# One comparison for four tokens' one-hot rows, and first products queued behind the gate products of their group

## The chip, the cores and the metric

The kernel runs on one core of a Trainium2 chip. The metric is the device time of one launch in microseconds (us). TensorE (PE) multiplies matrices, VectorE (DVE), ScalarE (ACT) and GpSimd (POOL) work on tiles of 128 partitions, and SyncE (SP) issues most of the DMAs.

## The reference, cut to what matters

The program is one step of a decoder layer for 512 prompt tokens and 64 sample tokens. Its first part (projections, a short convolution, windowed attention, a layer norm) is not touched. The part that matters is PEER: each token picks 8 x 16 of 16384 experts, and an expert's number is a pair of keys of 128 each.

```
idx  = cand_i[best]                                # key_a * 128 + key_b, 8 heads x 16 per token
gate = softmax(best_s)
pre  = einsum('nd,nhkd->nhk', xb, expert_u[idx])
coef = gate * gelu(pre)
out  = einsum('nhk,nhkd->nd', coef, expert_v[idx])
```

## The kernel before

The 576 tokens are split. Two tiles of tokens (GATHER) fetch their experts' rows one by one with indirect DMAs. This is the side work: `experts` yields after each of 385 steps, and a step issues a gather of 512 KB on POOL (line 511) and a multiply with a sum on DVE (line 525, tile `junk`; in the later half line 534). Three tiles of 128 tokens (DENSE, 384 tokens) are computed against all 16384 experts, 128 tiles of 128 experts each.

For the dense tokens there are three pieces of work:

- A **front** (function `front`) makes the first product of one expert tile: a 512 KB load, its split into a high and a low part (`whi` on ACT, `wlo` on POOL, lines 118 and 119, four buffers each), 24 matmuls of 384 columns (lines 122 to 124), and a GELU on ACT. For the first 60 tiles the result goes to DRAM (`spill`). Each split also paces the side work: 2, 1, 2, 1, ... steps per front.
- The **gate products** (`gate_matrix`) turn each token's 128 pairs of keys and gates into a matrix of 128 x 128. Keys and gates are transposed into `pt` (line 755), copied to `T`, and for each token two one-hot tiles are made: `oj` marks the second key, `oi` marks the first key times the gate. One matmul `oj` x `oi` (line 775) gives the token's matrix. Four tokens share a PSUM bank, which ACT copies out (line 776), and 16 tokens (a **group**) go to DRAM as `gd` (line 778). `ONE_HOT = "vvag"` lets DVE make `oj` for two of four tokens, ACT for one (two instructions, lines 769 and 770) and POOL for one; DVE makes every `oi` (line 774). `iota_ps` is the row 0 to 127 in PSUM.
- A **back** multiplies a front's result with the gate matrices (`gm` read from `gd`, `re` from `spill`), splits the product (`chi`, `clo`), and adds 18 matmuls to the sums `acc` (line 913).

The keys come out of two top-16 searches on DVE (`top16`, `route`, lines 413 to 472), tile by tile. 20 fronts are queued during these searches. Then 24 groups of gate products follow, and with them the next fronts: 46 of them in equal shares after each group, the last 3 of the first 69 (AHEAD) behind the last gate product. Then the loop over the 128 expert tiles starts: a back for each, and fronts again from the 70th on, which begin once 58 backs are queued. `gm` needs the `gd` of all groups.

Each engine runs its instructions in the order of its queue. The build's scheduler sets that order from its own estimate of times and from the dependences; `tc.issue_after(x)` puts the instructions that are written in its block behind x in the queue of x's own engine, and binds no other engine.

Of the kernel before, what the change touches and what calls it, by code (L numbers as in the profile page):

```python
# [17 lines left out]
AF = mybir.ActivationFunctionType  # L18
ALU = mybir.AluOpType
# [28 lines left out]
GN = 16  # L48
# [5 lines left out]
AHEAD = NS + LAG  # L54
# [1 line left out]
GLAG = 2  # L56
RAW = dict(w=3, v=3)
HI = dict(w=4, v=2)
OB = 10


ORDER = "qkscscasacsca"
FQ = 5
KEEP = 3
LAST = 2


PACE_N = 18
PACE_A, PACE_B, PACE_U, PACE_V = (1, 0), (2, 1, 1), (2, 1), (1, 3)
LO_N = 50  # L70
ONE_HOT = "vvag"


@with_exitstack
def step_kernel(ctx: ExitStack, tc: tile.TileContext, I: dict, O: dict):
    nc = tc.nc
    V, A, G, PE, S = nc.vector, nc.scalar, nc.gpsimd, nc.tensor, nc.sync
# [18 lines left out]
    def bank(tag):  # L96
        if tag == "u":
            return ps_u.tile([128, 512], F32, tag="u", name="ps")
        return pools[tag].tile([128, 512], F32, tag=tag, name="ps")

    def tmp(p, shape, tag, name=None, bufs=1, dt=F32):
        return pools[p].tile(shape, dt, tag=tag, name=name or tag, bufs=bufs)

    loads, newest = [], [None, None]
# [6 lines left out]
    def const(name, shape, dtype=F32, src=None):  # L111
        t = pools["c"].tile(shape, dtype, tag=name, name=name)
        if src is not None:
            loads.append((t, src))
        return t
# [59 lines left out]
    iota128 = const("iota128", [128, 128], src=I["iota128"])  # L175
# [576 lines left out]
    def gate_matrix(i, keys, gt, gd):  # L752
        pt = shared[0]
        for k, src in enumerate((*keys, gt)):
            PE.transpose(pt[:, k * 128:(k + 1) * 128], src, ident)
        iota_ps = pt[:, 384:512]
        T = tmp("k", [128, 3, 128], "T3")
        A.activation(T, pt[:, :384].rearrange("p (k n) -> p k n", k=3), AF.Copy)
        for g in range(128 // GN):
            gb = tmp("b", [128, 128, GN], "gb", bufs=2)  # L760
            for q in range(GN // 4):
                ps = bank("mm")
                for r in range(4):
                    n = g * GN + q * 4 + r
                    oj = tmp("b", [128, 128], "oj", bufs=OB)
                    oi = tmp("b", [128, 128], "oi", bufs=OB)
                    who = ONE_HOT[n % len(ONE_HOT)]
                    if who == "a":
                        A.activation(oj, iota128, AF.Abs, bias=T[:, 1, n:n + 1], scale=-1.0)
                        A.activation(oj, oj, AF.Relu, bias=1.0, scale=-1.0)  # L770
                    else:
                        eng, numbers = (V, iota_ps) if who == "v" else (G, iota128)
                        eng.tensor_scalar(oj, numbers, T[:, 1, n:n + 1], None, op0=ALU.is_equal)  # L773
                    V.tensor_scalar(oi, iota_ps, T[:, 0, n:n + 1], T[:, 2, n:n + 1], op0=ALU.is_equal, op1=ALU.mult)  # L774
                    newest[1] = PE.matmul(ps[:, r * 128:(r + 1) * 128], oj, oi, start=True, stop=True).ins  # L775
                A.activation(gb[:, :, q * 4:(q + 1) * 4].rearrange("p i n -> p n i"),
                             ps.rearrange("p (n i) -> p n i", n=4), AF.Copy)
            S.dma_start(gd[i * (128 // GN) + g], gb)
            yield g

# [48 lines left out]
    def front(t):  # L829
        wu = table(I["euT"][t], "w", G if t < AHEAD else V, PACE_U[t % len(PACE_U)] if t < AHEAD else 0)  # L830
        ps = bank("u")
        for k in range(8):
            mm3(ps[:, :ND], block(wu, k), (hT[0][:, k, :], hT[1][:, k, :]), k == 0, k == 7)
        if t < NS:
            ge = tmp("f", [128, ND], "sp", bufs=2)
            A.activation(ge, ps[:, :ND], AF.Gelu)  # L836
            S.dma_start(spill[t], ge)
        else:
            ge = tmp("f", [128, ND], "gel", bufs=LAG)
            A.activation(ge, ps[:, :ND], AF.Gelu)  # L840
            coef[t] = ge
# [3 lines left out]
    def fronts(n):  # L845
        nonlocal done
        while done < min(n, NE):
            front(done)
            done += 1
# [4 lines left out]
    total = len(DENSE) * 128 // GN  # L854
    base = done
    for i in range(len(DENSE)):
        for g in gate_matrix(i, *second.sel[i], gd):
            fronts(base + (AHEAD - KEEP - base) * (i * (128 // GN) + g + 1) // total)
    with tc.issue_after(newest[1]):
        fronts(AHEAD)  # L860
    bs.close()
# [137 lines left out]
def build(nc, arrays):  # L999
    ins = {k: nc.dram_tensor(f"in_{k}", v.shape, mybir.dt.from_np(v.dtype), kind="ExternalInput").ap()  # L1000
           for k, v in arrays.items()}
    outs = {k: nc.dram_tensor(f"out_{k}", s, F32, kind="ExternalOutput").ap() for k, s in _OUTS.items()}
    with tile.TileContext(nc, schedule_with_timeline_sim=True) as tc:
        step_kernel(tc, ins, outs)
# [20 lines left out]
```

## Time and profile before

| | us |
|---|---|
| median of 3 runs | 1916.29 (1912.41 to 1923.74) |
| the profiled execution | 1920.95 |
| its span in the trace | 1919.2 |
| PE busy in the span | 1752.2 (91%) |
| DVE busy | 1602.6 (84%) |
| POOL busy | 1119.8 (58%) |
| ACT busy | 808.8 (42%) |
| DMA, mean | 259 GB/s |

An engine's busy time counts its compute instructions. Matmuls overlap, so the busy share of PE is above its share of real work, and the step from one matmul's start to the next is the better price. Of the 1.75 us between the span and the execution's time nothing is shown in the trace.

### The profile page before, as it was taken

To read this page: it belongs to the slowest core of one execution; us is meant where nothing else is said; L and a number is where in the kernel's file an instruction comes from. 1 tells how busy PE (TensorE), PEld (TensorE's weight loads), DVE (VectorE), ACT (ScalarE), POOL (GpSimd) and SP (SyncE) were. 2 spreads that over 40 slices of the span, in tenths; PEclk is the share of its full clock that TensorE was granted. 3 is DMA by queue.
4 is the path that set the end of the run, shared out by engine and by line. 5 is a ranking of instruction groups with operands and counts; after the bars stand their busy time and mean duration, and the time that the engine had idled before them with its cause. 6 is when DMAs were issued, how large, how long until landed. Compare 5 with 4: busy or idle time off the path is not lost.

```text
span 1919.2 us, 28284 instructions
## 1 busy us (share of the span) xinstructions
PE 1752.2 (91%) x9760; PEld 1583.2 (82%) x9760; DVE 1602.6 (84%) x3208; ACT 808.8 (42%) x1283; POOL 1119.8 (58%) x724
## 2 busy tenths in 40 slices
PE   8999998988889878789998889999999999999985
PEld 7897897877689778789996677877899999999974
DVE  6646689997956999999999767778888788889888
ACT  4554343433333333466777433333333333343322
POOL 4445434366766656567995222222678777777783
PEclk9999999998989898899998899999999999999998
DMA  6435433347766668668997799999999999989983
GB/s 243 151 127 213 129 131 121 116 169 271 257 204 223 208 203 269 207 228 292 354 355 250 234 334 323 340 348 335 322 339 346 317 336 358 338 312 345 317 270 111
DMA packets 190303, 496.49 MB, mean 259 GB/s; under 512 B 17472, under 2 KB 83456, under 8 KB 187072
## 3 DMA queue, kind: packets, MB, share of 16 engines
q1 hardware_dynamic: 134864, 293.34, 44.5%
q0 software_dynamic: 55296, 201.35, 29.7%
q8 instruction: 77, 1.26, 0.3%
q14 instruction: 66, 0.54, 0.1%
HBM read 454.48 MB, written 40.54 MB: 258 GB/s over the span
## 4 chain that ended last, share of the span: by engine, by line
PE 38%; DVE 31%; DMA 14%; issue 8%; POOL 6%; ACT 2%; SPq 1%; DVEq 0%; POOLq 0%; ACTq 0%
PE acc L913 17%; PE ps L123 6%; PE ps L124 6%; PE ps L122 6%; DVE junk L525 4%; DVE oi L774 4%; POOL wlo L119 3%; POOL g L511 3%; DMA re<-spill 2%; DMA g<-in_eu,idx 2%; DMA g<-in_ev,idx 2%; PE ps L775 2%; DVE oj L773 1%; ACT whi L118 1%; DVE oh L469 1%
## 5 line engine op out<-in xcount | busy, mean ns | idle before, releaser
L119 POOL TENSOR_TENSOR wlo<-raw,whi 128x1024 fp32r<-128x1024 f32 x232 | 580.7, 2506 | 306.6 <-ACT whi L118 277.3
L118 ACT ACTIVATE whi<-raw 128x1024 fp32r<-128x1024 f32 x388 | 409.6, 1056 | 594.1 <-PE ps L123 231.8
L122 PE MATMUL ps<-xhi,whi 128*128 128x384 f32 (+2 forms) x1600 | 534.5, 334 | 24.8 <-ACT sp L836 22.9
L124 PE MATMUL ps<-xhi,wlo 128*128 128x384 f32 (+2 forms) x1600 | 531.9, 333 | 2.6 <-POOL wlo L119 2.6
L123 PE MATMUL ps<-xlo,whi 128*128 128x384 f32 (+2 forms) x1600 | 531.8, 332 | 0.0
L511 POOL DMA_INDIRECT g<-in_eu,idx x192 | 205.9, 1072 | 292.6 <-DVE junk L525 220.3
L534 DVE SCALAR_TENSOR_TENSOR h<-g,pre,h 128x1024 f32<-128x1024 f32 x192 | 315.3, 1642 | 64.8 <-DMA g<-in_ev,idx 63.3
L122 PEld LDWEIGHTS ps<-xhi,whi 128*128 128x128 f32 x1600 | 309.7, 194 | 32.4 <-ACT sp L836 24.5
L511 POOL DMA_INDIRECT g<-in_ev,idx x192 | 259.0, 1349 | 124.4 <-DVE h L534 77.1
L124 PEld LDWEIGHTS ps<-xhi,wlo 128*128 128x128 f32 x1600 | 309.3, 193 | 4.6 <-POOL wlo L119 3.4
L123 PEld LDWEIGHTS ps<-xlo,whi 128*128 128x128 f32 x1600 | 309.3, 193 | 4.3 <-issue 1.4
L913 PE MATMUL acc<-whi,chi 128*128 128x512 f32 x756 | 294.0, 395 | 16.1 <-ACT chi L118 16.1
L913 PE MATMUL acc<-wlo,chi 128*128 128x512 f32 x756 | 299.6, 396 | 6.2 <-POOL wlo L119 6.2
L119 DVE TENSOR_TENSOR wlo<-raw,whi 128x1024 fp32r<-128x1024 f32 x156 | 206.6, 1324 | 58.1 <-ACT whi L118 56.0
L913 PE MATMUL acc<-whi,clo 128*128 128x512 f32 x756 | 251.4, 392 | 2.1 <-DVE clo L119 2.1
L913 PEld LDWEIGHTS acc<-whi,chi 128*128 128x128 f32 x756 | 143.9, 190 | 48.4 <-ACT chi L118 19.7
L913 PEld LDWEIGHTS acc<-wlo,chi 128*128 128x128 f32 x756 | 144.0, 190 | 37.1 <-POOL wlo L119 8.3
L913 PEld LDWEIGHTS acc<-whi,clo 128*128 128x128 f32 x756 | 143.0, 189 | 32.7 <-DVE clo L119 2.7
L775 PE MATMUL ps<-oi,oj 128*128 128x128 f32 x768 | 145.1, 301 | 25.5 <-DVE oi L774 15.0
L775 PEld LDWEIGHTS ps<-oi,oj 128*128 128x128 f32 x768 | 127.9, 202 | 40.2 <-issue 10.6
L525 DVE SCALAR_TENSOR_TENSOR junk<-g,hp 128x1024 bf16<-128x1024 f32 x104 | 125.3, 1205 | 37.6 <-DMA g<-in_eu,idx 35.9
L774 DVE TENSOR_SCALAR oi<-pt,T 128x128 f32<-128x128 f32 x384 | 140.4, 395 | 0.1
(251 smaller groups left out, 2380.8 us busy)
## 6 DMA issues: line engine op xcount, KB each, us to landing
raw<-in_euT SPq DMA_DIRECT2D x128, 512.0 KB
raw<-in_ev SPq DMA_DIRECT2D x128, 512.0 KB
gd<-gb SPq DMA_DIRECT2D x24, 1024.0 KB
gm<-gd SPq DMA_DIRECT2D x48, 512.0 KB
raw<-in_w_g SPq DMA_DIRECT2D x32, 512.0 KB
raw<-in_w_pq SPq DMA_DIRECT2D x32, 512.0 KB
raw<-in_w_bch SPq DMA_DIRECT2D x24, 512.0 KB
spill<-sp SPq DMA_DIRECT2D x60, 192.0 KB
```

The source lines that it names most:

```text
L118: A.activation(hi, src, AF.Copy)
L119: return (eng or V).tensor_tensor(lo, src, hi.bitcast(F32), op=ALU.subtract)
L122: PE.matmul(ps, L[0], R[0], start=start, stop=False)
L123: PE.matmul(ps, L[0], R[1], start=False, stop=False)
L124: PE.matmul(ps, L[1], R[0], start=False, stop=stop)
L469: V.tensor_tensor(oh.rearrange("p h k a -> p (h k) a"), rk.unsqueeze(2).broadcast_to([r, 64, 16]), iota[:r].unsqueeze(1).broadcast_to([r, ...
L511: G.indirect_dma_start(out=rows[i], out_offset=None, in_=I[src], in_offset=bass.IndirectOffsetOnAxis(ap=idx[c][:, s:s + 1], axis=0))
L525: V.scalar_tensor_tensor(junk, g, 1.0, in_psum(c), op0=ALU.mult, op1=ALU.mult, accum_out=p)
L534: V.scalar_tensor_tensor(h_tok[c], g, p, h_tok[c], op0=ALU.mult, op1=ALU.add)
L774: V.tensor_scalar(oi, iota_ps, T[:, 0, n:n + 1], T[:, 2, n:n + 1], op0=ALU.is_equal, op1=ALU.mult)
L775: newest[1] = PE.matmul(ps[:, r * 128:(r + 1) * 128], oj, oi, start=True, stop=True).ins
L913: PE.matmul(*args, **kw)
```

## The change

For every four tokens one DVE comparison of 128 x 1024 makes all eight one-hot rows (`hot`: two keys, four tokens, 128 columns), in place of the one or two DVE instructions per token and the `oj` of ACT and POOL. The gate is then multiplied into the first-key row in place: by ACT for three of four tokens, by POOL for the fourth (`GATED`). DVE takes the copy out of PSUM of the last of a group's four banks (`OUT`). There are three `hot` buffers where there were ten of `oj` and of `oi`. The matmuls of a group's share of fronts stand behind that group's last gate product in PE's queue, and 8 of the first 69 fronts, not 3, stay behind the last gate product.

```diff
--- before.py
+++ after.py
@@ -56,19 +56,20 @@
 GLAG = 2
 RAW = dict(w=3, v=3)
 HI = dict(w=4, v=2)
-OB = 10
+OB = 3
 
 
 ORDER = "qkscscasacsca"
 FQ = 5
-KEEP = 3
+KEEP = 8
 LAST = 2
 
 
 PACE_N = 18
 PACE_A, PACE_B, PACE_U, PACE_V = (1, 0), (2, 1, 1), (2, 1), (1, 3)
 LO_N = 50
-ONE_HOT = "vvag"
+GATED = "aaag"
+OUT = "aaav"
 
 
 @with_exitstack
@@ -760,21 +761,24 @@
             gb = tmp("b", [128, 128, GN], "gb", bufs=2)
             for q in range(GN // 4):
                 ps = bank("mm")
+                n = g * GN + q * 4
+                hot = tmp("b", [128, 2, 4, 128], "hot", bufs=OB)
+                V.tensor_tensor(hot, iota_ps.unsqueeze(1).unsqueeze(1).broadcast_to([128, 2, 4, 128]),
+                                T[:, 0:2, n:n + 4].unsqueeze(3).broadcast_to([128, 2, 4, 128]), op=ALU.is_equal)
                 for r in range(4):
-                    n = g * GN + q * 4 + r
-                    oj = tmp("b", [128, 128], "oj", bufs=OB)
-                    oi = tmp("b", [128, 128], "oi", bufs=OB)
-                    who = ONE_HOT[n % len(ONE_HOT)]
-                    if who == "a":
-                        A.activation(oj, iota128, AF.Abs, bias=T[:, 1, n:n + 1], scale=-1.0)
-                        A.activation(oj, oj, AF.Relu, bias=1.0, scale=-1.0)
+                    oi = hot[:, 0, r, :]
+                    weight_of = T[:, 2, n + r:n + r + 1]
+                    if GATED[r] == "a":
+                        A.activation(oi, oi, AF.Copy, scale=weight_of)
                     else:
-                        eng, numbers = (V, iota_ps) if who == "v" else (G, iota128)
-                        eng.tensor_scalar(oj, numbers, T[:, 1, n:n + 1], None, op0=ALU.is_equal)
-                    V.tensor_scalar(oi, iota_ps, T[:, 0, n:n + 1], T[:, 2, n:n + 1], op0=ALU.is_equal, op1=ALU.mult)
-                    newest[1] = PE.matmul(ps[:, r * 128:(r + 1) * 128], oj, oi, start=True, stop=True).ins
-                A.activation(gb[:, :, q * 4:(q + 1) * 4].rearrange("p i n -> p n i"),
-                             ps.rearrange("p (n i) -> p n i", n=4), AF.Copy)
+                        G.tensor_scalar(oi, oi, weight_of, None, op0=ALU.mult)
+                    newest[1] = PE.matmul(ps[:, r * 128:(r + 1) * 128], hot[:, 1, r, :], oi, start=True, stop=True).ins
+                dst = gb[:, :, q * 4:(q + 1) * 4].rearrange("p i n -> p n i")
+                src = ps.rearrange("p (n i) -> p n i", n=4)
+                if OUT[q] == "a":
+                    A.activation(dst, src, AF.Copy)
+                else:
+                    V.tensor_copy(dst, src)
             S.dma_start(gd[i * (128 // GN) + g], gb)
             yield g
 
@@ -855,7 +859,8 @@
     base = done
     for i in range(len(DENSE)):
         for g in gate_matrix(i, *second.sel[i], gd):
-            fronts(base + (AHEAD - KEEP - base) * (i * (128 // GN) + g + 1) // total)
+            with tc.issue_after(newest[1]):
+                fronts(base + (AHEAD - KEEP - base) * (i * (128 // GN) + g + 1) // total)
     with tc.issue_after(newest[1]):
         fronts(AHEAD)
     bs.close()
```

Three places show what moves. In the order of the program the line numbers after the change are one higher, as far as the gate products.

The first place is PE's queue at the first gate products (`pt` the transposed keys, `oi`, `oj` and `hot` one-hot tiles, 128x384 the matmuls of fronts). Before:

```order
3893 L775 MATMUL ps<-oi,oj 128x128
3894 L122 MATMUL ps<-xhi,whi 128x384
3895 L123 MATMUL ps<-xlo,whi 128x384
3896 L124 MATMUL ps<-xhi,wlo 128x384
3897 L775 MATMUL ps<-oi,oj 128x128 x3
3898 L122 MATMUL ps<-xhi,whi 128x384
3899 L775 MATMUL ps<-oi,oj 128x128
3900 L123 MATMUL ps<-xlo,whi 128x384
3901 L124 MATMUL ps<-xhi,wlo 128x384
3902 L122 MATMUL ps<-xhi,whi 128x384
3903 L775 MATMUL ps<-oi,oj 128x128 x2
```

And in the changed program, from the end of the 20th front on:

```order
3609 L124 MATMUL ps<-xlo,whi 128x384
3610 L125 MATMUL ps<-xhi,wlo 128x384
3611 L756 MATMUL pt<-ident,kk_5506 128x128
3612 L756 MATMUL pt<-ident,kk_5507 128x128
3613 L756 MATMUL pt<-ident,gt 128x128
3614 L775 MATMUL ps<-hot 128x128 x16
3615 L123 MATMUL ps<-xhi,whi 128x384
3616 L124 MATMUL ps<-xlo,whi 128x384
3617 L125 MATMUL ps<-xhi,wlo 128x384
```

Before, 30 of the 69 fronts stand ahead of the last transposes of the first tile, and gate products come singly between the matmuls of fronts. Now 20 fronts stand ahead of them, and the 16 gate products of a group stand together. The further counts are 49 fronts before and 31 now ahead of the second tile's transposes, and 65 and 45 ahead of the third's.

The second place is PE's queue at the last gate products. Before:

```order
4914 L775 MATMUL ps<-oi,oj 128x128
4915 L123 MATMUL ps<-xlo,whi 128x384
4916 L124 MATMUL ps<-xhi,wlo 128x384
4917 L775 MATMUL ps<-oi,oj 128x128 x126
4918 L122 MATMUL ps<-xhi,whi 128x384
4919 L123 MATMUL ps<-xlo,whi 128x384
4920 L124 MATMUL ps<-xhi,wlo 128x384
```

And in the changed program:

```order
4579 L124 MATMUL ps<-xlo,whi 128x384
4580 L125 MATMUL ps<-xhi,wlo 128x384
4581 L775 MATMUL ps<-hot 128x128 x10
4582 L123 MATMUL ps<-xhi,whi 128x384
4583 L124 MATMUL ps<-xlo,whi 128x384
4584 L125 MATMUL ps<-xhi,wlo 128x384
```

Before, 126 gate products of the third tile stand in one piece and 3 fronts behind them; now the last piece is 10 gate products, with 10 fronts behind it (8 kept and the share of the last group). Behind these fronts the 58 backs follow in both.

The third place is DVE's queue in the third tile (`junk` is a step of the side work). Before:

```order
1642 L773 TENSOR_SCALAR oj<-pt,T_10343 128x128
1643 L774 TENSOR_SCALAR oi<-pt,T_10343 128x128
1644 L773 TENSOR_SCALAR oj<-pt,T_10343 128x128
1645 L774 TENSOR_SCALAR oi<-pt,T_10343 128x128 x3
1646 L773 TENSOR_SCALAR oj<-pt,T_10343 128x128
1647 L774 TENSOR_SCALAR oi<-pt,T_10343 128x128
1648 L773 TENSOR_SCALAR oj<-pt,T_10343 128x128
1649 L774 TENSOR_SCALAR oi<-pt,T_10343 128x128 x3
1650 L773 TENSOR_SCALAR oj<-pt,T_10343 128x128
1651 L774 TENSOR_SCALAR oi<-pt,T_10343 128x128
1652 L773 TENSOR_SCALAR oj<-pt,T_10343 128x128
1653 L774 TENSOR_SCALAR oi<-pt,T_10343 128x128
```

And in the changed program:

```order
1267 L766 TENSOR_TENSOR hot<-pt,T_9521 128x1024 x2
1268 L781 COPY gb<-ps 128x4x128
1269 L766 TENSOR_TENSOR hot<-pt,T_9521 128x1024
1270 L526 SCALAR_TENSOR_TENSOR junk,pre<-g,hp 128x1024 x2
1271 L766 TENSOR_TENSOR hot<-pt,T_9521 128x1024 x3
1272 L526 SCALAR_TENSOR_TENSOR junk,pre<-g,hp 128x1024
1273 L781 COPY gb<-ps 128x4x128
1274 L766 TENSOR_TENSOR hot<-pt,T_9521 128x1024
1275 L526 SCALAR_TENSOR_TENSOR junk,pre<-g,hp 128x1024 x2
1276 L766 TENSOR_TENSOR hot<-pt,T_9521 128x1024 x3
1277 L526 SCALAR_TENSOR_TENSOR junk,pre<-g,hp 128x1024
```

Six instructions for four tokens became one; the copy of `gb` waits for the last gate products of its group on PE. Of the side work's DVE steps 77 stand ahead of the first tile's last key reduction before and 69 now; 136 and 125 stand ahead of the last one-hot instruction.

## Rows read from the trace of the kernel before

**Rows 1.** Busy time by stretch: us, PE, PEld, DVE, ACT, POOL, PEclk, DMA share, GB/s.

```profile
727.00:783.00 56.00, 43.45 (x237) 42.50 (x236) 56.00 (x167) 17.45 (x24) 36.21 (x25) 0.92 0.79 259
783.00:913.00 130.00, 117.49 (x711) 113.93 (x712) 130.00 (x339) 80.22 (x138) 90.38 (x71) 0.94 0.73 245
913.00:1008.00 95.00, 95.00 (x640) 95.00 (x639) 90.92 (x251) 71.87 (x129) 86.55 (x77) 1.00 0.96 355
1008.00:1081.00 73.00, 60.03 (x298) 48.87 (x297) 71.02 (x216) 52.98 (x105) 35.12 (x45) 0.88 0.63 227
1081.00:1353.00 272.00, 256.08 (x1113) 210.95 (x1112) 202.69 (x304) 94.83 (x125) 68.69 (x62) 0.97 0.96 333
```

**Rows 2.** Timeline: start us, us, instruction. The marks that end those stretches.

```profile
726.89 0.47 ACT L836 ACTIVATE sp<-ps 128x384 f32<-128x384 f32 x1
...
783.20 0.42 PE L755 MATMUL pt<-ident,gt 128*128 128x128 f32 x1
...
1096.67 0.80 PE L913 MATMUL acc<-whi,chi 128*128 128x512 f32 x1 [3.60 <-ACT chi L118]
...
1353.39 0.33 PE L122 MATMUL ps<-xhi,whi 128*128 128x384 f32 x1
```

**Rows 3.** Timeline of PE: two matmuls 24 apart, and one at the low clock.

```profile
784.38 0.52 PE L122 MATMUL ps<-xhi,whi 128*128 128x384 f32 x1
...
1084.07 0.33 PE L122 MATMUL ps<-xhi,whi 128*128 128x384 f32 x1
...
1088.23 0.33 PE L122 MATMUL ps<-xhi,whi 128*128 128x384 f32 x1
```

**Rows 4.** Timeline of PE: one gate product between two matmuls of a front.

```profile
987.64 0.42 PE L123 MATMUL ps<-xlo,whi 128*128 128x384 f32 x1
987.90 0.39 PE L775 MATMUL ps<-oi,oj 128*128 128x128 f32 x2
988.04 0.42 PE L124 MATMUL ps<-xhi,wlo 128*128 128x384 f32 x1
```

**Rows 5.** Chain that ended last: start us, us. One back's matmuls.

```profile
1707.04 4.12 PE acc L913 x18
```

**Rows 6.** Timeline of PE in the third tile; idle time before, and its releaser, in brackets.

```profile
1058.11 5.51 PE L775 MATMUL ps<-oi,oj 128*128 128x128 f32 x24 [1.00 <-DVE oi L774]
```

**Rows 7.** Groups by line and form: busy us, mean ns | idle before.

```profile
L774 DVE TENSOR_SCALAR oi<-pt,T 128x128 f32<-128x128 f32 x384 | 140.4, 395 | 0.1
L773 DVE TENSOR_SCALAR oj<-pt,T 128x128 f32<-128x128 f32 x192 | 64.2, 334 | 0.9 <-issue 0.9
L773 POOL TENSOR_SCALAR oj<-iota,T 128x128 f32<-128x128 f32 x96 | 63.8, 667 | 40.0 <-PE ps L775 38.7
L769 ACT ACTIVATE oj<-iota,T 128x128 f32<-128x128 f32 x96 | 36.1, 377 | 13.8 <-PE ps L775 13.6
L770 ACT ACTIVATE oj<-oj 128x128 f32<-128x128 f32 x96 | 29.5, 310 | 2.6
L776 ACT ACTIVATE gb<-ps 128x512 f32<-128x512 f32 x96 | 101.6, 1059 | 52.5 <-PE ps L775 48.4 <-issue 2.5 <-PE ps L123 1.6
```

**Rows 8.** Stretches, side-work steps on DVE (L525) alone; two records each.

```profile
783.00:913.00 130.00, 23.44 (x39) 0.94 0.73 245
...
1008.00:1081.00 73.00, 12.94 (x22) 0.88 0.63 227
```

**Rows 9.** Lines L469 and L305 of DVE: ns min/median/max.

```profile
L469 DVE TENSOR_TENSOR oh<-rk,iota x20: 1195/1206/4082, 300.9 to 895.4; 128x1024 bf16<-128x1024 f32 x16, 64x1024 bf16<-64x1024 f32 x4
...
L305 DVE COPY t<-ps x8: 407/666/692, 106.5 to 439.6; 128x512 f32<-128x512 f32 x6, 64x256 f32<-64x256 f32 x2
```

**Rows 10.** Timeline: first and last of six long DVE instructions, and the POOL instruction beside the first.

```profile
740.52 2.88 DVE L457 CAST pf<-pos 128x128 bf16<-128x128 uint32 x1
740.91 2.39 POOL L119 TENSOR_TENSOR wlo<-raw,whi 128x1024 fp32r<-128x1024 f32 x1
...
774.81 3.21 DVE L469 TENSOR_TENSOR oh<-rk,iota 128x1024 bf16<-128x1024 f32 x1
```

## The prediction

> **What bounds the kernel now.** I read the busy times by stretch first, cut at the marks of [rows 2]: 727, where PE is done with the 20th front; 783, the first tile's last transpose; 913 and 1008, the same for the second and third tile; 1081, the last gate product; and 1353, where PE reaches the 70th front. What lies ahead of 727 and behind 1353 has the same queues before and after, so I forecast only how 1353 moves. In [rows 1] no engine bounds all five stretches: DVE is full up to 913, PE and DMA (0.96, 355 GB/s) up to 1008, DVE alone up to 1081, and DMA (0.96) with PE after that. The question in each stretch is how much of it is PE's own work, since PE's work as a whole (49 fronts, 384 gate products, 58 backs) is the same after the change.
>
> Prices on PE: a front is 24 matmuls, and two starts 24 matmuls apart lie 4.16 us apart [rows 3], 0.173 us each. From the start of a front's matmul over a gate product to the next start it is 0.40 us [rows 4], so a gate product costs 0.227 us. A back is 4.12 us [rows 5]. With the counts of fronts from PE's queue, PE's idle or slow time in the five stretches before is:
>
> - 727 to 783: 56 less 10 fronts (41.6) = 14.4.
> - 783 to 913: 130 less 19 fronts (79.0) and 128 gate products (29.1) = 21.9.
> - 913 to 1008: 95 less 16 fronts and 128 products (95.7) = 0.
> - 1008 to 1081: 73 less 1 front and 128 products (33.2) = 39.8. Here PE waits for one-hot tiles of DVE again and again [rows 6].
> - 1081 to 1353: 272 less 3 fronts and 58 backs (12.5 + 239.0) = 20.5.
>
> That is 97 us together. The change can only move this number.
>
> **The change, part by part.**
>
> *One comparison for eight rows.* In the third tile DVE is busy 71.0 us, 12.9 of them for side work [rows 1, 8], so the one-hot tiles take 58.1 us there, 0.454 us a token or 1.82 us for four (less than the mean durations of [rows 7] add up to, since DVE's instructions overlap). A `hot` is not in the trace. The nearest row is the comparison of 128 x 1024 with both operands broadcast, 1.206 us [rows 9]; it reads SBUF alone, and `hot` reads one operand from PSUM. Bounds: 1.1 (0.1 of the row's time saved by overlap) and 1.82 (no gain at all). I take 1.2. So DVE saves 0.6 us for four tokens, 59 us over 96 of them.
>
> *The copies that DVE takes over.* 24 of 96. DVE's copy of the same size out of PSUM takes 0.69 us [rows 9]; ACT's, which writes with the stride of `gb`, 1.06 [rows 7]. Bounds 0.6 and 1.2, taken 0.7: 17 us back on DVE.
>
> *The multiplies.* On POOL 96 multiplies replace 96 comparisons of the same 128 x 128 form at 0.667 us [rows 7]: taken as no change, bounds 0.6 and 0.9. On ACT 288 multiplies with a scale from a column replace 96 pairs of 0.377 and 0.310 us. Between 0.31 and 0.377 each they take 89 to 109 us; less the 66 of the pairs and 25 of the 24 copies, ACT gains or loses between -2 and +18 us. Its cover: ACT was busy 71.9 of 95 us in the busiest stretch [rows 1]. Without cover it would be all of it, 18 us.
>
> *The fronts behind their group.* This moves PE's work and with it loads, splits and side steps. Stretch by stretch:
>
> (a) 727 to the first transposes. PE has only fronts there, and now they may not pass the gate products. So PE stands still from 727 until DVE has the first tile's keys, and DVE decides when that is: it is busy all of the 56 us [rows 1]. Two things leave its way. Eight side steps go behind (77 against 69 in its queue); one costs 23.4 us over some 20 = 1.2 [rows 8], so 9.6 us. And POOL's `wlo` instructions stop once the four buffers are full, since PE frees none. While a `wlo` runs, certain DVE instructions take 2 to 3 us in place of 0.2 to 1.2: the first of them starts just before a `wlo` and ends with it [rows 10]. I count six such in this stretch behind the fourth buffer, 13.5 us over their usual durations. So the keys come at 783 - 9.6 - 13.5 = 760, and PE's idle time is 33 us. Bounds: 28 (DVE also overtakes for want of the other stalls) and 42 (no stall saved but four).
>
> (b) The first tile, 760 on. DVE must still finish the searches. Before it used 130 - 23.4 - 128 x 0.454 = 48.6 us for them in this stretch [rows 1, 8]. Now: 48.6 + 32 `hot` (38.4) + 8 copies (5.6) + 15 side steps (18) = 110.6. PE has 11 fronts and 128 products, 74.9 us, so it idles 36. Bounds 25 (fewer stalls by `wlo`, 11 against about 20) and 50 (`hot` at 1.5 us).
>
> (c) The second and third tile. Now PE has 28 fronts and 256 products, 174.6 us. DVE has 64 x 1.2 + 16 x 0.7 + 41 side steps x 1.2 = 137 us, POOL does for each front and product what it did from 913 to 1008, where it was busy 86.6 of 95 us, and DMA's load is near that of the same stretch. PE should bound this stretch, as it did that one with POOL at 91% and DMA at 0.96 [rows 1]. Its queue is less forgiving, though: no front may fill a wait for the last four tokens of a group. I give it half a microsecond a group, 8 us. Bounds 0 and 30.
>
> So the last gate product lies at 760 + 111 + 183 = 1054, 27 us ahead of 1081.
>
> (d) From there to the 70th front. Ten fronts instead of three: 41.6 + 239.0 = 280.6 us of PE. That covers the way from the last `gd` to the first back, on which PE stood 3.6 us [rows 2] and lost its clock. But DMA is the bound of this stretch: 272 us at 333 GB/s. Seven more fronts' tables and eleven more gathers (136 against 125 steps ahead of the last one-hot instruction), 0.524 MB each, are 9.4 MB or 28 us at that rate, 300 in all if nothing of it was fetched ahead. Between 281 and 300 I take 294: PE idles 13, bounds 1 and 20.
>
> Sum of idle time after: 33 + 36 + 8 + 13 = 90 against 97. The gain is 7 us. Of the 40 us that PE wins back in the third tile most is paid in (a) and (b), where fronts no longer fill the wait for DVE. Against the profiled 1920.95 us this makes 1914; that execution lies 0.24% above the median, so the median comes to 1916.3 x 1914/1920.95 = 1909 us. My own range for this case is 1897 to 1918.
>
> **A rule beside it.** In [rows 3] a matmul takes 0.52 us, not 0.33, right after PE's wait for the transposes: the lower of the two clock levels, 1.2 for 2.4 GHz. In the third tile, where PE got a product every half microsecond, the granted clock stayed at 0.88 [rows 1]. The Trainium skill, "TensorE: Matmul & The Clock Gate", Part 1, says that the slow clock is the default state and that only activity releases it. By that rule a first tile with PE idle a third of the time would run its fronts slow throughout; by the row of the third tile it would not, and the sum goes by the row.
>
> **The rivals.**
>
> 1. *Slower: the last four tokens of each group wait.* The fourth token's multiply stands on POOL behind up to one `wlo` of 2.4 us [rows 10], and PE's fronts stand behind it. At 2.4 us for each of the 16 groups of (c), 38 us in place of 8: 1939. It decides from about 1 us a group on. For it: POOL is 91% busy in the comparable stretch, and three `hot` buffers instead of ten leave little lead. Against: PE runs one or two fronts, 4 to 8 us, between groups, in which three `hot` can be made ready.
> 2. *Slower: the clock falls in (b).* Eleven fronts at twice 4.16 us and products at twice 0.227 make 150 us of PE in place of 111 of DVE, from the point where PE's slow work exceeds DVE's: 1948 in full, some 1930 for half of it. Against: 0.88 in the third tile.
> 3. *Faster: DVE is quicker and DMA no bound.* The stalls by `wlo` shrink in (b) as in (a) and idle time is 25 there, 0 in (c), 2 in (d), 30 in (a): 57, a gain of 40, 1876; half of that 1890. For it: DMA stood at 0.63 in the third tile and at 0.84 just behind it, and could fetch ahead. Against: DMA's 0.96 for 272 us.
> 4. *No change: DMA takes all.* The stretch (d) needs 300 us and nothing is won: 1915.
>
> **How the numbers follow.** A difference under 0.5%, some 9.6 us, is about what a measurement of this kernel cannot tell from none. The forecast case gets 0.43, a little under half of it beyond 0.5% (0.20 faster, 0.23 same). Rival 3 gets 0.22, faster. Rival 4 gets 0.13, same. Rival 1 gets 0.16 and rival 2 0.06, slower. So 0.42 faster, 0.36 same, 0.22 slower. The range of 8 in 10 cuts the far half of rival 3 and the far part of rivals 1 and 2: 1884 to 1935.
>
> **What would show it.** Right: PE without a matmul from 727 to about 760; the first tile's transposes at 760 and the second tile's near 870, with DVE full between; a `hot` near 1.2 us, also while a `wlo` runs; the last gate product near 1054; then 42 us of fronts and the first back without a gap; the 70th front near 1347; DMA at 0.95 or more for the last 290 us of that. Wrong: waits of PE for ACT's or POOL's multiplies in the second and third tile of more than a microsecond a group (rival 1); a granted clock under 0.8 in the first tile (rival 2); DMA well below 0.95 behind the last gate product (rival 3); a `hot` of 1.5 us and more, which adds 10 us in (b) alone.

## The result, and the profile after

The changed kernel takes 1985.03 us (1982.0 to 1992.02, 4 runs) where the kernel before takes 1914.35 on the same chip: a ratio of 1.0382, 95% interval 1.0357 to 1.0407. It is slower by 3.8%, and the prediction, 1909 us, was wrong in sign. The profiled execution took 1983.27 us, its span 1981.5.

Line numbers of the changed program: `hot` is made in L766, the gate is multiplied in by ACT in L772 and by POOL in L774, the product is L775, the copies are L779 (ACT) and L781 (DVE); the lines of the fronts lie one higher than before. The stretches are cut much as in [rows 1], with two differences. The first cut stays at 727 although the mark itself, the spill of the 20th front, lies earlier here, at 720. And the second and third tile are cut at 868 and 992, where the last gate products of the tile ahead end, 4 us behind their transposes (864 and 988). The other cuts are the first tile's transposes (750), the last gate product (1116) and the 70th front.

The busy time by stretch of the changed kernel (us, PE, its weight loads PEld, DVE, ACT, POOL, granted clock of PE, DMA share, GB/s; x counts instructions):

```profile
727.00:750.00 23.00, 0.47 (x1) 0.18 (x1) 23.00 (x115) 0.26 (x1) 0.00 (x0) 0.50 0.06 23
750.00:868.00 118.00, 92.44 (x523) 89.47 (x523) 93.15 (x177) 70.67 (x148) 62.94 (x59) 0.84 0.54 196
868.00:992.00 124.00, 101.98 (x595) 99.65 (x595) 69.19 (x81) 69.64 (x149) 73.40 (x69) 0.92 0.67 238
992.00:1116.00 124.00, 102.01 (x593) 99.86 (x594) 70.16 (x84) 70.01 (x149) 73.27 (x68) 0.91 0.68 241
1116.00:1412.70 296.70, 286.49 (x1286) 242.27 (x1286) 219.59 (x328) 105.13 (x141) 98.01 (x80) 0.98 0.99 344
```

Its timeline has the mark that ends the last of them, the 70th front:

```profile
1412.73 0.33 PE L123 MATMUL ps<-xhi,whi 128*128 128x384 f32 x1
```

Against 1353.39 in [rows 2] that is 59 us later; with 569 us behind the mark (566 before) this is the whole loss of 62 us between the spans. In the two tiles from 868 to 1116 no engine is full: PE 0.82, DVE 0.56, ACT 0.56, POOL 0.59, DMA 0.67. A stretch in which nothing is full is one in which the engines wait for each other in turn. The waits of this stretch say in which order (us in total, times, longest):

```profile
ACT hot L772 <- DVE hot L766: 58.2, 18, 5.5
...
DVE hot L766 <- PE ps L775: 46.5, 11, 6.5
...
PE ps L775 <- ACT hot L772: 40.6, 20, 3.2
...
PE ps L775 <- POOL hot L774: 3.6, 3, 1.2
```

ACT's multiply waits for DVE's comparison, that one for a product of PE, and PE's product for ACT's multiply: a ring. Before, DVE's one-hot instructions waited 1.0 us in all [rows 7]. One turn of it, a group of 16 tokens, on the three engines. PE (fronts left out):

```profile
911.21 1.50 PE L775 MATMUL ps<-hot 128*128 128x128 f32 x12
915.56 4.22 PE L775 MATMUL ps<-hot 128*128 128x128 f32 x20 [2.85 <-ACT hot L772]
```

DVE:

```profile
903.05 1.05 DVE L781 COPY gb<-ps 128x512 f32<-128x512 f32 x1 [1.40 <-PE ps L775]
903.95 1.21 DVE L766 TENSOR_TENSOR hot<-pt,T 128x1024 f32<-128x1024 f32 x1
...
911.70 3.49 DVE L766 TENSOR_TENSOR hot<-pt,T 128x1024 f32<-128x1024 f32 x3 [4.14 <-PE ps L775]
```

ACT:

```profile
912.56 2.78 ACT L779 ACTIVATE gb<-ps 128x512 f32<-128x512 f32 x3
915.14 2.69 ACT L772 ACTIVATE hot<-hot,T 128x128 f32<-128x128 f32 x9
```

A product leaves two records, so PE does 6 products, stands 2.85 us, and does 10. The names with their numbers in PE's queue say which (four `hot` to a group: 8820 to 8856, then 8908 and on; 48 rows of fronts stand at the first dots, 24 at the second):

```
L775 MATMUL ps_8819<-hot_8820 128x128 x3
L775 MATMUL ps_8831<-hot_8832 128x128 x3
...
L775 MATMUL ps_8819<-hot_8820 128x128
L775 MATMUL ps_8831<-hot_8832 128x128
L775 MATMUL ps_8843<-hot_8844 128x128 x4
L775 MATMUL ps_8855<-hot_8856 128x128 x3
L775 MATMUL ps_8907<-hot_8908 128x128 x3
L775 MATMUL ps_8919<-hot_8920 128x128 x3
L775 MATMUL ps_8855<-hot_8856 128x128
...
L775 MATMUL ps_8907<-hot_8908 128x128
```

The first three tokens of `hot` 8820 and 8832 have their products ahead of the share of fronts that is queued behind the group before, the fourth (the one that POOL multiplies) has its product behind it. With three buffers the fourth `hot`, 8856, takes the buffer of 8820, so DVE can only make it when the fronts are over (911.70), and the first two of the next group with it. ACT copies three banks before it multiplies, PE waits, and no front may fill the wait, since the next share is queued behind the group.

### The profile page after: what moved, and what is told of

It reads as the page before. It is cut to its first block, busy times and chain, and to the rows that moved or that the text cites. A ratio compares the mean times of both kernels' runs of the same rounds, so it can differ in the third digit from the quotient of the medians.

```text
span 1981.5 us, 27705 instructions
## 1 busy us (share of the span) xinstructions
PE 1758.6 (89%) x9760; PEld 1597.2 (81%) x9760; DVE 1520.5 (77%) x2752; ACT 807.6 (41%) x1353; POOL 1123.9 (57%) x724
## 5 line engine op out<-in xcount | busy, mean ns | idle before, releaser
L512 POOL DMA_INDIRECT g<-in_ev,idx x192 | 268.5, 1398 | 119.6 <-DVE h L535 72.5
L775 PE MATMUL ps<-hot 128*128 128x128 f32 x768 | 126.7, 327 | 69.0 <-ACT hot L772 65.4
L775 PEld LDWEIGHTS ps<-hot 128*128 128x128 f32 x768 | 118.2, 227 | 76.1 <-ACT hot L772 71.7
L766 DVE TENSOR_TENSOR hot<-pt,T 128x1024 f32<-128x1024 f32 x96 | 113.1, 1212 | 68.1 <-PE ps L775 58.7
```

Source lines behind the costliest of these rows:

```text
L512: G.indirect_dma_start(out=rows[i], out_offset=None, in_=I[src], in_offset=bass.IndirectOffsetOnAxis(ap=idx[c][:, s:s + 1], axis=0))
L766: V.tensor_tensor(hot, iota_ps.unsqueeze(1).unsqueeze(1).broadcast_to([128, 2, 4, 128]), T[:, 0:2, n:n + 4].unsqueeze(3).broadcast_to([128 ...
L775: newest[1] = PE.matmul(ps[:, r * 128:(r + 1) * 128], hot[:, 1, r, :], oi, start=True, stop=True).ins
```

## The experiments

Each ratio is against the kernel before, run on the same chip beside it.

**Which part of the change costs: the queueing or the comparisons.** Fronts free again, in the changed kernel:

```diff
-            with tc.issue_after(newest[1]):
-                fronts(base + (AHEAD - KEEP - base) * (i * (128 // GN) + g + 1) // total)
+            fronts(base + (AHEAD - KEEP - base) * (i * (128 // GN) + g + 1) // total)
```

> The changed kernel without the queueing of each share of fronts behind its group (8 fronts still kept for the end). Theory A (PE waits about 2.5 us in each group of the second and third tile for the last four tokens, because three hot buffers hold their comparison back until PE has begun the group, and no front may fill that wait): the waits stay but fronts fill them, and fronts fill 727 to 750 again; the stretch from the first tile's transposes to the last gate product shrinks and the time falls by 40 to 70 us, to 1915 to 1945. Theory B (ACT's queue holds the multiplies back behind three copies out of PSUM, whatever PE does meanwhile): with all fronts free to go first they run early and the third tile is left to the gate products alone, as before the change; the time falls by less than 30 us, to 1955 or more.

Measured: 1889.96 us (1886.2 to 1895.61), ratio 0.987 (0.9825 to 0.9916), faster than either theory had it. The same with `KEEP = 3`, so that only the gate products' change is left:

> Only the new one-hot rows: no queueing of the fronts, 3 fronts kept as before. Theory A: the third tile's products stand nearly alone at the end as before the change, at a round trip of about 10 us for 16 tokens there; the saved DVE time (0.6 us for four tokens) shows up to the second tile; 1905 to 1930. Theory C (the queueing is what costs, the one-hot rows gain what they save on DVE, 59 us in all, about 25 of them in the third tile): 1885 to 1900.

Measured: 1897.99 us (1890.98 to 1902.44), ratio 0.9929 (0.99 to 0.9958). The other way round, the one-hot tiles of before with their ten buffers, and the change's queueing and `KEEP = 8`:

```diff
-OB = 3
-GATED = "aaag"
-OUT = "aaav"
+OB = 10
+ONE_HOT = "vvag"
...
-                V.tensor_tensor(hot, iota_ps.unsqueeze(1).unsqueeze(1).broadcast_to([128, 2, 4, 128]),
-                                T[:, 0:2, n:n + 4].unsqueeze(3).broadcast_to([128, 2, 4, 128]), op=ALU.is_equal)
...
+                    V.tensor_scalar(oi, iota_ps, T[:, 0, n:n + 1], T[:, 2, n:n + 1], op0=ALU.is_equal, op1=ALU.mult)
```

> The one-hot rows of before (ten buffers of oj and oi) with the fronts queued behind their group and 8 kept. Theory A: ten buffers let the one-hot tiles of the next group be made while PE runs fronts, so no wait of 2 us and more in the second and third tile; DVE needs 7.3 us for 16 tokens and 3 for side steps, under PE's 11; idle time is only that ahead of the first tile's end; 1910 to 1935. Theory C (queueing fronts behind gate products costs, however the one-hot rows are made): 1960 to 1990.

Measured: 1943.62 us (1934.58 to 1951.05), ratio 1.0142 (1.0089 to 1.0194), between the ranges of the two theories. The comparisons alone gain 0.7%, the queueing alone loses 1.4%, and together they lose 3.8%: the two interact. Where fronts are free, PE still meets late multiplies. The view of the product's line lists what PE and its weight loads, counted apart, waited for ahead of it (us, times). The changed kernel:

```profile
  ACT hot L772: 137.1, 62
  POOL hot L774: 7.7, 6
```

The first of these three kernels:

```profile
  ACT hot L772: 61.9, 63
  POOL hot L774: 4.7, 7
```

As many waits, less than half as long, since the scheduler put fronts beside them. In the kernel with the queueing alone the second and third tile (866 to 1080) take 214 us, between the 183 forecast and the 252 that the changed kernel takes from its transposes on. PE waits there 21 us in all, for copies, ACT, POOL and DVE in turn, never longer than 2.2 us. Its ten buffers, too, are fewer than the 16 tokens of a group; that this is the reason there is an argument, not a run.

**Buffers.** Five `hot` in place of three, room for them taken by letting the score tiles use the same buffers earlier on; the queueing as in the changed kernel:

```diff
-OB = 3
+OB = 5
...
-            sc = tmp("kb"[s.w], [128, 4, 128], "sc", bufs=2 + s.w * 2)[:s.rows[i]]
+            sc = (tmp("b", [128, 2, 4, 128], "hot", bufs=OB)[:, 0] if s.w else tmp("k", [128, 4, 128], "sc", bufs=2))[:s.rows[i]]
```

> The changed kernel with five hot buffers in place of three (the space comes from the score tiles, which use the same buffers ahead of the gate products). Theory A: a whole group's four comparisons and multiplies can be ready when PE comes to it; PE's waits for hot in the second and third tile fall from 44 us to under 10, the granted clock there rises from 0.92 to 0.98 and more; the time falls by 50 to 70 us, to 1915 to 1935, near what was predicted for the change. Theory B (ACT's queue): buffers do not matter, the waits stay above 30 us, 1970 to 1990.

Measured: 1891.14 us (1889.24 to 1897.11), ratio 0.9894 (0.9846 to 0.9941). The transposes of the second tile lie at 836.6 and the last gate product at 1021.4, so the second and third tile take 185 us, where 183 were predicted. The time lies below the range that was expected, since the first tile got shorter too: its transposes lie at 751, so it takes 86 us, in place of 114. The same view of the product's line as above:

```profile
  ACT gb L779: 20.9, 14
  ACT hot L772: 8.1, 6
```

The 137.1 us became 8.1. Fewer buffers, `OB = 2`:

> The changed kernel with two hot buffers. Theory A: two of a group's four quarters now wait for a round trip over PE, DVE and ACT, so PE's waits for hot in the second and third tile grow from 44 us to 80 and more, with more time at the low clock; 2030 to 2100. Theory B (ACT's queue order alone): with fewer multiplies made ahead no more than a few us a tile, 1980 to 2010.

Measured: 1983.42 us (1980.35 to 1988.6), ratio 1.0385 (1.0361 to 1.041), the same as with three, where theory A had 2030 and more. So it isn't that each buffer takes off a part. Its waits from 868 to 1116:

```profile
PE ps L775 <- ACT hot L772: 24.7, 16, 1.6
...
PE ps L775 <- POOL hot L774: 16.0, 13, 2.3
```

That is 41 us, with three buffers it was 44; now it comes in two pieces a group. In this kernel no product stands on the wrong side of the fronts: a group's 16 products (16, 12 and 4 records, from 896.25 to 903.9 in one of them) stand together between two shares. The odd order of the changed kernel is not needed for the loss. And `OB = 4`, as many as a group has:

> The changed kernel with four buffers for the comparisons instead of three (their room shared with the score tiles), as many as a group has. Theory 'threshold at a group' (all four comparisons of the next group can be made while TensorE works through the fronts behind this one): TensorE's waits for multiplies in the stretch of the second and third tile fall under 15 us, that stretch takes 185 to 195 us, and the time is 1890 to 1910 us. Theory 'each buffer takes off a part' (or the buffers freed by a group's last products come too late): the waits fall by a third to a half only, and the time is 1930 to 1960 us.

Measured: 1897.24 us (1889.06 to 1899.5), ratio 0.9894 (0.987 to 0.9918). The step lies between three and four. With four the order on PE changes too, to 16 products in one piece; that two buffers have that order and lose all the same speaks for the buffers. Its second and third tile by stretch, and one whole group on PE:

```profile
844.00:939.00 95.00, 89.03 (x584) 87.77 (x582) 70.69 (x86) 71.32 (x153) 73.53 (x69) 0.98 0.87 312
939.00:1035.00 96.00, 92.20 (x621) 91.82 (x620) 69.14 (x83) 73.42 (x153) 75.54 (x69) 0.98 0.87 315
```

```profile
855.16 3.73 PE L775 MATMUL ps<-hot 128*128 128x128 f32 x32
```

16 products in 3.73 us without a gap, 0.233 us each, in place of 8.6 us with one. DVE beside it:

```profile
857.79 3.48 DVE L766 TENSOR_TENSOR hot<-pt,T 128x1024 f32<-128x1024 f32 x3
861.18 1.05 DVE L781 COPY gb<-ps 128x512 f32<-128x512 f32 x1
862.07 1.22 DVE L766 TENSOR_TENSOR hot<-pt,T 128x1024 f32<-128x1024 f32 x1
```

All four `hot` are made without a wait, by 863.3; the next group's first product comes at 867.1.

**The queue of the engine that multiplies.** The copies of a group's first three quarters moved from ACT to DVE (`OUT = "vvva"`), three buffers:

> The changed kernel, three hot buffers, but the first three copies out of PSUM of each group on DVE and the fourth on ACT. In the changed kernel ACT's queue has a group's three copies (2.8 us) ahead of the multiplies of its last four tokens. Theory B (those copies make up most of PE's 2.8 us of waiting per group): the last four tokens' chain is then one copy and one comparison on DVE and a multiply, 2.7 us, which PE's first three quarters of the group cover; waits for hot in the second and third tile fall from 44 us to under 20, time 1925 to 1950. Theory A in its bare form (three buffers alone: the last comparison cannot begin before PE begins the group, wherever the copies are): waits stay at 35 us or more, 1970 to 2000.

Measured: 1986.64 us (1985.96 to 1999.18), ratio 1.0411 (1.0387 to 1.0434): no gain. The waits from 868 to 1116:

```profile
DVE gb L781 <- PE ps L775: 63.2, 14, 6.2
PE ps L775 <- ACT hot L772: 32.8, 35, 1.2
```

The copies now wait for PE in DVE's queue and hold up the comparisons behind them. PE's waits for multiplies fell into shorter pieces and add up to 38 us, with those for POOL, in place of 44. In the next one the copies stay on ACT, but the second and third stand behind the group's last multiplies:

```diff
...
+                        mult = A.activation(oi, oi, AF.Copy, scale=weight_of)
...
+                if q in (1, 2):
+                    later.append((dst, src))
+                    continue
...
+                    with tc.issue_after(mult.ins):
+                        for d, s in later:
+                            A.activation(d, s, AF.Copy)
```

> Three buffers, and the copies of a group's second and third quarter on ScalarE are made to stand behind that group's last multiplies; the first copy stays ahead, since the fourth comparison needs its buffer only. Theory 'order of ScalarE's queue' (the nine late multiplies are late because 2.8 us of copies stand ahead of them): TensorE's wait for the ScalarE multiply in the stretch of the second and third tile falls from about 2.8 to about 1 us a group, that stretch from 248 to some 215 us, and the time to 1945 to 1960 us. Theory 'the loop through fewer buffers than a group has comparisons' (product, comparison, multiply, product again, whatever stands beside it): the wait stays above 2 us a group or moves to the copies, and the time stays at 1970 to 1990 us.

Measured: 1977.69 us (1974.47 to 1979.33), ratio 1.0323 (1.0306 to 1.034). ACT's queue did change, and PE's wait only split in two (its lines lie one higher):

```profile
895.55 1.50 PE L776 MATMUL ps<-hot 128*128 128x128 f32 x12
898.15 1.07 PE L776 MATMUL ps<-hot 128*128 128x128 f32 x6 [1.10 <-ACT hot L773]
900.68 3.33 PE L776 MATMUL ps<-hot 128*128 128x128 f32 x14 [1.47 <-ACT hot L773]
```

First for the fourth `hot`, then, behind the two copies, for the first of the next group, whose products the scheduler put ahead of the share. So ACT's copies alone do not make the wait. What was left to try was the order, products on the wrong side of the fronts. The last two kernels put a group's 16 products in one piece, with three buffers still: once by giving POOL the first of four tokens, once by giving it none.

```diff
-GATED = "aaag"
+GATED = "gaaa"
```

> Three buffers as in the changed kernel; POOL multiplies the first of each four tokens instead of the fourth, so each engine has the same work. In TensorE's queue of the changed kernel the fourth products of a group's first two fours stand behind the share of fronts, and ten of the sixteen products behind the wait; with POOL's token first the sixteen stand together. Theory 'order of the products': a group's first buffer comes free 0.9 us after the group's start, the fourth comparison and its multiplies need some 1.2 + 0.4 us behind it with two copies beside them, while TensorE has 2.7 us of products; its wait falls from 2.85 to under 1 us a group, the second and third tile take 190 to 210 us in place of 248, the time is 1895 to 1930 us. Theory 'fewer buffers than a group has comparisons': the fourth comparison still stands behind a product of its own group, the wait stays above 2 us a group, and the time at 1965 to 1990 us.

Measured: 1995.49 us (1985.77 to 2001.02), ratio 1.0453 (1.0386 to 1.0519). A miss for the first theory, although the products do stand in one piece: PE now does 12 of the 16 products in one run and waits 3.75 us for POOL in nearly every group. First PE, then POOL in one of them:

```profile
892.80 2.84 PE L775 MATMUL ps<-hot 128*128 128x128 f32 x24
899.38 0.91 PE L775 MATMUL ps<-hot 128*128 128x128 f32 x3 [3.75 <-POOL hot L774]
```

```profile
893.95 2.38 POOL L120 TENSOR_TENSOR wlo<-raw,whi 128x1024 fp32r<-128x1024 f32 x1 [0.60 <-ACT whi L119]
896.47 0.95 POOL L512 DMA_INDIRECT g<-in_eu,idx  x1
897.73 0.94 POOL L512 DMA_INDIRECT g<-in_eu,idx  x1 [0.30 <-DVE hot L766]
898.71 1.77 POOL L774 TENSOR_SCALAR hot<-hot,T 128x128 f32<-128x128 f32 x3
```

The fourth `hot` is ready near 895.2; POOL is in a `wlo` until 896.3 and issues two gathers of the side work before it comes to the multiply at 898.7.

```diff
-GATED = "aaag"
+GATED = "aaaa"
```

> Three buffers; ScalarE multiplies all four tokens of a comparison (96 multiplies of 0.39 us more on it, 12.5 us a tile, and none on POOL). The sixteen products of a group stand together in TensorE's queue, but all three copies of a group stand ahead of the fourth's multiplies on ScalarE. Theory 'order of the products': the wait falls to about 1.5 us a group (the third copy ends 3.8 us behind the group's start, the products ahead of it 2.7), the second and third tile take 205 to 220 us, the time is 1915 to 1945 us, above that with POOL's token first. Theory 'fewer buffers than a group has comparisons': 1965 to 1995 us as before.

Measured: 1930.03 us (1924.34 to 1930.89), ratio 1.0102 (1.0039 to 1.0165). With three buffers this is 2.7% better than the changed kernel (1.0102 by 1.0382), and a typical group waits 0.71 us (three of them 4.35 to 5.01):

```profile
882.79 2.84 PE L775 MATMUL ps<-hot 128*128 128x128 f32 x24
886.34 1.35 PE L775 MATMUL ps<-hot 128*128 128x128 f32 x8 [0.71 <-ACT hot L772]
```

Its second and third tile, from 846 to 1061, take 215 us. The two kernels have the same order on PE and differ by 3.5%, so the order alone does not decide; and as the second also takes POOL out of the ring, its gain cannot be put down to the order. What decides there is an argument from these rows, not a run of its own: with three buffers the fourth comparison starts when its group's first four products are done, and from there PE has eight more products, under 2 us, to hide the comparison (1.2 us) and whatever stands ahead of the multiply on the engine that makes it.

**The best of both.** Five buffers and the fronts free, with 8 and with 3 kept for the end:

> Five hot buffers and no queueing of the fronts, 8 kept. If the waits for hot and the idle stretch ahead of the first transposes are both worth their PE time, this beats five buffers alone by part of the 24 us that PE stands still from 727 to 751: 1870 to 1888. If DMA behind the last gate product takes what is won (0.99 busy there in all runs): 1885 to 1895, no better than either alone.

Measured: 1873.52 us (1864.96 to 1875.7), ratio 0.9805 (0.9779 to 0.983).

> As the kernel above with 3 fronts kept in place of 8. The 8 kept fronts cover the way from the last gate matrix to the first back: without them PE idles some 10 us there, but the last gate product and with it the DMA-bound stretch come no earlier; 5 to 10 us slower than with 8 if PE counts there, equal within 3 us if DMA alone does: 1880 to 1898.

Measured: 1871.02 us (1864.91 to 1888.12), ratio 0.9814 (0.9778 to 0.9851). Both beat both kernels; how many fronts are kept makes no difference that these runs can tell.

## Why the prediction was wrong

**Step (c), the second and third tile, failed.** It gave "half a microsecond a group", 183 us from the second tile's transposes on; measured were 252 us (864 to 1116), 69 more. The whole error at the 70th front is 65 us (1412.7 against 1347 to 1348): the transposes of the first tile came 10 us early, (b) and (d) took 3 us more each. The four-buffer kernel does the same work in 191 us. Against the 248 us from 868 on, 57 us lie between them and can be taken apart. PE's waits for multiplies in the changed kernel are 44.2 us by the rows above; with four buffers the waits ahead of the product are these:

```profile
PE ps L775 <- ACT gb L779: 9.0, 5, 3.2
PE ps L775 <- ACT hot L772: 0.6, 1, 0.6
```

That is 35 us. The products' own busy time (us, PE, PEld, clock, DMA share, GB/s), first in the changed kernel, then with four buffers:

```profile
868.00:1116.00 248.00, 82.48 (x513) 77.13 (x514) 0.91 0.67 240
```

```profile
844.00:1035.00 191.00, 63.18 (x520) 61.21 (x520) 0.98 0.87 314
```

That is 19 us, most of it the clock: behind a wait PE runs largely at the lower level, 10 products in 4.22 us at a granted clock of 0.60 (915.6 to 919.4), against 16 in 3.73 us at 1.00 with four buffers. Some 3 us are left. So the term of 8 us for waits should have been 44, and the clock, which stood at 0.91 against 0.98 with four buffers, had no term in (c) at all. Against the prediction's own 175 us of PE's work four buffers, too, take 7 us beyond their waits; that was not taken apart. The Trainium skill, "TensorE: Matmul & The Clock Gate", Part 1, has the slow clock as the default state and activity as what releases the fast one; the trace agrees, with 0.50 in the stretch where PE stands still and about 0.9 where it stands for 2.85 us in most groups. The first tile, at 0.84, was not slow throughout.

**Rival 1 was the right mechanism, with a wrong argument against it.** It said that the last four tokens of a group would wait, and at more than a microsecond a group would decide. It was dismissed because three `hot` can be made ready between groups. Three were made, exactly as said; a group has four, and the fourth needs a buffer that PE gives back only in the same group. The rival's price, 38 us, lies near the 44 measured by luck: it took POOL's `wlo` for the cause. In the changed kernel the late multiply stands behind ACT's three copies, 2.78 us (moving two of them away split the wait and did not remove it), and with POOL's token first it stood behind POOL's `wlo` and gathers. It also left out the clock.

**Step (a) was right, but its start was not.** PE stood empty until the first transposes, which came at 750, not 760. The prediction took what lies ahead of 727 as unmoved; in this execution the mark of [rows 2], 726.89, came at 720.31:

```profile
720.31 0.47 ACT L840 ACTIVATE sp<-ps 128x384 f32<-128x384 f32 x1
...
743.90 0.47 PE L756 MATMUL pt<-ident,kk 128*128 128x128 f32 x1 [24.46 <-DVE kk L473]
750.04 0.48 PE L756 MATMUL pt<-ident,kk 128*128 128x128 f32 x1 [5.67 <-DVE kk L473]
```

So PE idled 30 us, where 33 were predicted, and 7 of the 10 us came from ahead of the stretch; why that part was quicker stays open. POOL has no instruction from 727 to 750, so no `wlo` was there to hold DVE up.

**Step (b) came out near for a wrong reason.** 111 us with DVE full were predicted; it took 114 up to the transposes at 864, with DVE busy 93.15 of them. DVE needs less than the sum said, and the ring takes the rest: with four buffers the stretch took 94 us with DVE full (92.93). The clock, 0.84, stayed above the 0.8 at which rival 2 would have begun.

**Step (d) was right:** 297 us against 294, with DMA at 0.99 and 344 GB/s. Rival 4's argument, that DMA sets this stretch, holds with four buffers too: 296.

**Prices.** The groups by line (busy us, mean ns, idle before), to be set beside [rows 7]:

```profile
L775 PE MATMUL ps<-hot 128*128 128x128 f32 x768 | 126.7, 327 | 69.0 <-ACT hot L772 65.4 <-POOL hot L774 3.6
...
L766 DVE TENSOR_TENSOR hot<-pt,T 128x1024 f32<-128x1024 f32 x96 | 113.1, 1212 | 68.1 <-PE ps L775 58.7 <-ACT whi L119 9.0 <-ACT T L759 0.4
L772 ACT ACTIVATE hot<-hot,T 128x128 f32<-128x128 f32 x288 | 90.5, 394 | 89.2 <-DVE hot L766 88.7
...
L774 POOL TENSOR_SCALAR hot<-hot,T 128x128 f32<-128x128 f32 x96 | 58.5, 620 | 111.9 <-DVE hot L766 108.3 <-DVE rk L468 2.8
L781 DVE COPY gb<-ps 128x512 f32<-128x512 f32 x24 | 25.0, 1043 | 30.4 <-PE ps L775 30.4
```

`hot` was priced right (1.2 us). ACT's multiply, 394 ns, lies above its bound of 377, DVE's copy at 1.04 us near the top of its bounds, not at 0.7. Neither made the error: with five buffers, at the same prices (392 and 1044 ns), (c) took 185 us.

What stays open: why two buffers cost just what three do (41 and 44 us of waits, in other places) was seen but not taken apart.

## What to carry to other kernels

Count a tile's buffers against what one block of the waiting engine's queue uses: if other work is queued in order behind a block of four, three buffers make the fourth's chain of producers run with that engine idle, and four let it run behind the other work. A pool that was large enough while the scheduler could fill gaps isn't any more once work is tied to an order, so change the two together. And read the order of the consumer's instructions, not only their number: one late product of a buffer's four kept the buffer for a whole share of fronts. But an order without late products did not help by itself: two buffers had it, and three with POOL's token first, and both lost as much.

## What the runs showed of the hardware that was not expected

The comparison out of PSUM never stalled: over 96 `hot` the shortest took 1181 ns and the longest 1225, also with a `wlo` on POOL, where the long instructions of [rows 10] took 2 to 3 us. DVE's copy into the stride of `gb` took 1.04 us where its copy of the same size in [rows 9] took 0.67, much as ACT's strided copy, 1.06. And standing still cost PE more than the wait: 35 us more of it in two tiles brought 19 us more of slow products.
